# A decoder block in fp32 on one core: V transposed by VectorE instead of TensorE, and a seven-product block multiplication that sums in PSUM

## The chip, the cores and the metric

The kernel runs on one core of one Trainium2 chip. The metric is device time in microseconds for one launch that computes the whole block; lower is better. The core has five engines with instruction queues of their own: TensorE (PE, with its weight loads shown apart as PEld), VectorE (DVE), ScalarE (ACT), GpSimd (POOL) and SyncE (SP), which here does nothing but issue transfers. Each engine works through its own queue in order, and waits on semaphores for the others.

## What is computed

One decoder block on a sequence of 2048 positions with 1024 channels, everything float32. The largest part is one input projection into 9216 columns; its columns are q, k and v of a dilated attention in three groups, several gates, and the input of a linear recurrence (RG-LRU).

```python
proj = x @ w_in[l] + b_in[l]                       # (2048 x 1024) @ (1024 x 9216)
q, k, v, g_attn, u_lru, g_lru, gate_logits = jnp.split(proj, SPLIT_POINTS, axis=-1)
q = rope(...); k = rope(...)
for g, (window, dilation) in enumerate(DILATION_GROUPS):
    o_g, lse_g = dilated_band_attention(q[:, :, g], k[:, :, g], v[:, :, g], window, dilation)
...
y_a = (attn * silu(g_attn)) @ w_attn_proj[l]
h = rg_lru(causal_depthwise_conv(u_lru, ...), ...)
y_b = (h * jax.nn.silu(g_lru)) @ w_lru_proj[l]
merged = gates[:, :, 0] * y_a + gates[:, :, 1] * y_b
x = layer_norm(DEEPNORM_ALPHA * x + merged @ w_out[l] + b_out[l], ...)
```

## The kernel before

The program has three stages, one after the other. Stage A is the input projection, stage B the attention, stage C the three output products and the normalisation. The change lies in stage A.

**Number format.** Every fp32 operand of a product is split into a high and a low part (`h`, `l` for weights, planes 0 and 1 of the activation blocks `XB`), and each block product is three passes, high by high, high by low, low by high.

**Quads and products.** Stage A takes the 72 column tiles of 128 in 36 pairs, and the sequence in two halves of two chunks of 512 positions (`CH`). One pair in one half is a *quad*; there are 72. In a quad a 2x2 block of weights meets a 2x2 block of activations, with seven block products instead of eight (Strassen's scheme in Winograd's form), called M1 to M7 below after the numbers of `UNIT` and `BLK`. Only the first quad of each half multiplies plainly, with eight. A block product is one *tick*: `product(s, j)` issues 12 matmuls of 128x128 by 128x512 into one PSUM bank. `MID`, `EDGE` and `FIRST` give the order of the seven in a quad. All 506 ticks are issued by one loop, and this loop writes the order of all engines by hand: in each tick the product, then the `events` due (loads, splitting of weights three or four ticks ahead in `prep_w`, sums of weights), then delayed pieces (`late`), then steps of the chains, and last `evacuate(s, j)`, which deals with the bank just finished.

**Sums of the products.** The four results of a quad are, up to signs, M1+M2, U2+M5+M3, U2+M7+M5 and U2+M7+M4 with U2 = M1-M6. In the kernel before, each product has a bank to itself (tag `q`, four banks), ACT copies M1 to SBUF as `e`, and DVE makes everything else: `u2 = e - M6`, `u3 = u2 + M7`, then in `result` and `total` the four results (`y`, or `ub` for the recurrence), and once more `u2 = u2 + M5`. The banks of a quad are read by seven DVE instructions.

**Chains.** What happens to a result is a generator that advances by steps, each step once its engine has time left by a planner's account (`Ask`, `spend`, `COST`). `qk_chain` turns q and k; its four small transfers `sw` (line 307) swap partition quarters, and for the third group q is written at line 341 in pieces of 32 numbers, 128 bytes. `v_chain` has to turn V from channels on partitions to positions on partitions. It asks PE for four transposes against an identity matrix (`turn`, line 358) into a PSUM tile `vtp` (tag `t`, two banks); they are issued in the middle of a product, by `pe_later`. Three ticks on, ACT copies the tile to one of two SBUF buffers `vs` (line 366), and a tick later SP stores it with one transfer (line 370) to `v_scr`, in pieces of 128 numbers. There are 48 such chains, four in each of 12 quads. Stage B reads `v_scr` back with positions on partitions.

The eight PSUM banks of stage A are four `q`, two `t` and two `g` (gates of the recurrence).

**End of stage A.** The last quad also issues the first loads of stage B, in the slots that its blocks free: `first` (keys and queries of unit 0, in the slots of M1's and M2's blocks), `second` (unit 1, in those of M6 and M4), `firstv` (V, in that of M7).

Of the kernel before, what the change touches and what calls it, by code (L numbers as in the profile page):

```python
# [8 lines left out]
F32 = mybir.dt.float32  # L9
# [22 lines left out]
def hybrid_block_kernel(ctx: ExitStack, tc: tile.TileContext, a: dict, out: bass.AP):  # L32
# [89 lines left out]
    MID, EDGE, FIRST = (1, 6, 7, 5, 2, 4, 3), (1, 2, 6, 7, 4, 5, 3), (1, 2, 3, 6, 7, 5, 4)  # L122
# [89 lines left out]
    def hi_lo(n, kk, src, eng=dve):  # L212

        t = XB[n][:, kk]
        act.activation(t[:, 0], src, AF.Copy)  # L215
        eng.tensor_tensor(out=t[:, 1], in0=src, in1=flat(t[:, 0]), op=ALU.subtract)
# [131 lines left out]
    vs_free = [sl_p.tile([P, 4, P], F32, name=f"vs{j}") for j in range(2)]  # L348
    tog = {"n": 0}

    def v_chain(vt, sgn, f, c):
        g, hp = divmod(f - FT_V, 4)
        st = {}

        def turn():
            tp = st["tp"] = ps.tile([P, 4, P], F32, tag="t", name=f"vtp{f}_{c}", bufs=2)
            for b in range(4):
                pe.transpose(tp[:, b, :], flat(vt)[:, b * P:(b + 1) * P], ident)  # L358
            give(vt)

        yield Ask(cond=lambda: tog["n"] < 2)
        tog["n"] += 1
        pe_later(2, turn)
        yield Ask(lag=3, cond=lambda: len(vs_free) > 0, ACT=.66)
        vs = vs_free.pop(0)
        act.activation(vs, st["tp"], AF.Copy, scale=sgn)
# [3 lines left out]
        sp.dma_start(dst.rearrange("(b p) f -> p b f", p=P), vs)  # L370
        vs_free.append(vs)
# [26 lines left out]
    def silu_chain(y, sgn, f, c):  # L398
# [3 lines left out]
        act.activation(y, y, AF.Identity, scale=0.25 * sgn, bias=bq[:, f:f + 1])  # L402
# [153 lines left out]
    for h in range(2):  # L556
        for p, (kind, f0, f1) in enumerate(seq):
            plan.append((h, ((f0, kind), (f1, kind)), None if p == 0 else EDGE if p == len(seq) - 1 else FIRST if p == 1 else MID, p, kind))
    NQ = len(plan)
    ticks = [8 if pl[2] is None else 7 for pl in plan]  # L560
    base = [sum(ticks[:s]) for s in range(NQ + 1)]
# [45 lines left out]
    def product(s, j):  # L607
# [8 lines left out]
        bank = Q["b"]  # L616
# [975 lines left out]
```

## Time and profile before

| | us |
|---|---|
| median of 3 runs | 2104.6 (2103.72 to 2107.59) |
| profiled execution, first to last instruction (span) | 2101.9 |
| profiled execution's own time outside the span | not given; the median lies 2.7 above the span |
| first matmul of stage A starts | 5.97 |
| stage A ends on PE (first scores of stage B) | 1443.70 |
| busy in the span: PE, DVE, ACT, POOL | 2086.3, 1662.7, 1116.7, 493.1 |

Of the profile these views are used: the page, with its busy times and the chain that ended last; the waits, which say for each engine whom it waited for and how long in total; groups of instructions by line with busy time and mean duration; the timeline, where each row is a start, a duration, an engine and what it did, equal neighbours merged (x2 is two of them); and one tile's or one line's instructions with the least, median and largest duration. Matmuls are pipelined: the duration of one is longer than the distance to the next, so their cost is read from the distances of starts. Line numbers are those of the kernel before.

### The profile page before, as it was taken

The page shows a single profiled execution, that of the slowest core. Times are in us where ns is not written, and L with a number is a line of the kernel's source. Part 1 is how long each engine was busy: PE and PEld are TensorE (multiplying, and loading weights), DVE is VectorE, ACT ScalarE, POOL GpSimd, SP SyncE. Part 2 cuts the span into 40 slices and gives each one's busy share as a digit, 9 for nine tenths or more (in the row PEclk, how much of TensorE's full clock was granted, in tenths as well). Part 3 has the DMA queues.
Part 4 walks back from the last instruction along what each step waited for, and adds up shares of the span by engine and source line. Part 5 has one row for each costly group of instructions (what it writes and reads, how often), then busy time and mean ns, then how long its engine had stood idle before and what let it go on. Part 6 is the DMA issues. An engine that isn't in the chain of part 4 may idle for free.

```text
span 2101.9 us, 35814 instructions
## 1 busy us (share of the span) xinstructions
PE 2086.3 (99%) x12016; PEld 1726.9 (82%) x12016; DVE 1662.7 (79%) x3179; ACT 1116.7 (53%) x2341; POOL 493.1 (23%) x468
## 2 busy tenths in 40 slices
PE   8999999999999999999999999999999999999998
PEld 7888888888888888888888888888999888888887
DVE  8987888889988867787877888877999645576667
ACT  6455456457457565666666775766999411211100
POOL 1111111110111011231221222222545344431120
PEclk9999999999999999999999999999999999999999
DMA  8987997987997967777779778769996788864432
GB/s 271 276 261 225 274 285 216 282 283 235 278 294 242 332 208 204 231 227 220 225 254 278 254 252 266 252 219 374 355 359 236 228 296 281 298 224 160 154 105 71
DMA packets 327160, 524.69 MB, mean 250 GB/s; under 512 B 105536, under 2 KB 135232, under 8 KB 323136
## 3 DMA queue, kind: packets, MB, share of 16 engines
q1 hardware_dynamic: 307088, 489.54, 70.5%
q0 software_dynamic: 12256, 19.42, 5.5%
q10 hardware_dynamic: 7632, 13.44, 1.7%
q8 instruction: 96, 1.57, 0.3%
q14 instruction: 88, 0.72, 0.1%
HBM read 317.14 MB, written 190.45 MB: 241 GB/s over the span
## 4 chain that ended last, share of the span: by engine, by line
PE 91%; DVE 3%; DMA 3%; ACT 2%; issue 1%; SPq 0%; DVEq 0%; ACTq 0%
PE q L622 66%; PE yb L1340 3%; PE yb L1341 3%; PE z L1451 3%; PE yb L1342 3%; PE z L1450 3%; PE z L1452 3%; ACT p L1023 2%; DVE p L1015 2%; PE ya L1419 1%; PE ya L1418 1%; PE ya L1420 1%; PE g L492 1%; PE vtp L358 1%; DMA B<-k_scr 1%; DMA o_scr<-ot 1%
## 5 line engine op out<-in xcount | busy, mean ns | idle before, releaser
L622 PE MATMUL q<-xT,hS 128*128 128x512 f32 x1680 | 521.0, 391 | 0.0
L622 PE MATMUL q<-xT,l 128*128 128x512 f32 x1120 | 436.0, 389 | 0.0
L622 PE MATMUL q<-xB,hA 128*128 128x512 f32 x1248 | 388.9, 393 | 6.0 <-ACT xB L215 6.0
L622 PEld LDWEIGHTS q<-xT,hS 128*128 128x128 f32 x1680 | 312.9, 188 | 69.0 <-issue 5.5
L622 PE MATMUL q<-xB,l 128*128 128x512 f32 x904 | 352.9, 390 | 0.0
L622 PEld LDWEIGHTS q<-xB,hA 128*128 128x128 f32 x1248 | 233.8, 189 | 57.3 <-ACT xB L215 6.0
L622 PEld LDWEIGHTS q<-xT,l 128*128 128x128 f32 x1120 | 210.2, 188 | 44.1
L622 PEld LDWEIGHTS q<-xB,l 128*128 128x128 f32 x904 | 170.3, 188 | 36.0
L245 POOL DMA_DIRECT2D wS<-in_w_in_dram x70 | 61.9, 950 | 491.5 <-DMA wS<-in_w_in_dram 140.0
L622 PE MATMUL q<-xB,hS 128*128 128x512 f32 x560 | 174.0, 392 | 0.0
L1023 ACT ACTIVATE p<-p,sta 128x256 f32<-128x256 f32 (+1 forms) x384 | 172.7, 469 | 1.2 <-PE pt L1034 0.8
L622 PE MATMUL q<-xT,hA 128*128 128x512 f32 x560 | 173.0, 390 | 0.0
L269 ACT ACTIVATE hA<-wA 128x512 fp32r<-128x512 f32 x218 | 134.9, 623 | 54.4 <-DMA wA<-in_w_in_dram 24.9
L269 ACT ACTIVATE hS<-S 128x512 fp32r<-128x512 f32 x175 | 109.0, 623 | 79.3 <-DVE S L227 49.0
L227 POOL TENSOR_TENSOR S<-S,wA 128x512 f32<-128x512 f32 x35 | 45.5, 1301 | 391.8 <-DVE S L227 208.8
L622 PEld LDWEIGHTS q<-xT,hA 128*128 128x128 f32 x560 | 104.7, 188 | 23.0 <-issue 1.5
L622 PEld LDWEIGHTS q<-xB,hS 128*128 128x128 f32 x560 | 104.0, 188 | 22.4 <-issue 1.5
L1015 DVE CUSTOM_DVE_ANT_0 p<-s,mask 128x256 f32<-128x256 f32 (+1 forms) x384 | 116.4, 360 | 0.2 <-PE s L1008 0.2
L1451 PE MATMUL z<-wo,mh 128*128 128x512 f32 (+1 forms) x264 | 101.0, 383 | 0.0
L1452 PE MATMUL z<-wo,ml 128*128 128x512 f32 (+1 forms) x264 | 101.0, 383 | 0.0
L1450 PE MATMUL z<-wo,mh 128*128 128x512 f32 (+1 forms) x264 | 101.0, 383 | 0.0
L227 DVE TENSOR_TENSOR l<-wA,hA 128x512 fp32r<-128x512 f32 x113 | 79.3, 702 | 26.9 <-ACT hA L269 26.6
(204 smaller groups left out, 4257.0 us busy)
## 6 DMA issues: line engine op xcount, KB each, us to landing
wA<-in_w_in_dram SPq DMA_DIRECT2D x253, 256.0 KB, 4.7
wl_scr<-l SPq DMA_DIRECT2D x105, 512.0 KB, 5.2
l<-wl_scr SPq DMA_DIRECT2D x105, 512.0 KB, 4.6
sw<-y SPq DMA_DIRECT2D x384, 64.0 KB, 3.2
wS<-in_w_in_dram SPq DMA_DIRECT2D x70, 256.0 KB, 4.8
wS<-in_w_in_dram POOLq DMA_DIRECT2D x70, 256.0 KB, 6.3
qh_scr<-hi SPq DMA_DIRECT2D x48, 256.0 KB, 5.5
v_scr<-vs SPq DMA_DIRECT2D x48, 256.0 KB, 4.4
```

What stands on the lines that cost most here:

```text
L227: eng.tensor_tensor(out=out, in0=in0, in1=in1, op=op)
L245: pool.dma_start(t, w_part(s, x), accum_op=ALU.add)
L269: act.activation(h, r, AF.Copy)
L622: pe.matmul(bank, w[:, ks], x[:, kk, xx], start=(first and i == 0), stop=(last and i == 11))
L1015: dve.tensor_tensor_reduce(out=st["p", i, j][:, h, lo:256], in0=st["s", i, j // 2][h][:, j % 2, lo:256], in1=mask[:, lo:256], scale=1.0, s ...
L1023: act.activation(p, p, AF.Exp, scale=-1.0, bias=s[:, h:h + 1], accum_out=s[:, 2 + h:3 + h])
L1340: pe.matmul(yb, WL[f][:, 0, k], xx[:, 0], start=(k == 0), stop=False)
L1341: pe.matmul(yb, WL[f][:, 0, k], xx[:, 1], start=False, stop=False)
L1342: pe.matmul(yb, WL[f][:, 1, k], xx[:, 0], start=False, stop=(k == 7))
L1450: pe.matmul(z, mh[:, k], w[:, 0, hs], start=(k == 0), stop=False)
L1451: pe.matmul(z, mh[:, k], w[:, 1, hs], start=False, stop=False)
L1452: pe.matmul(z, ml[:, k], w[:, 0, hs], start=False, stop=(k == 7))
```

## The change

Three things change.

1. V is turned by VectorE. `v_chain` now transposes the result tile in 32x32 blocks with one DVE instruction into `vs`, without PE, PSUM or ACT. Since each block is turned in its own place, the store puts the blocks in order: four transfers for each V tile, one for each quarter of the partitions, in pieces of 32 numbers. So that no sign has to be applied on the way, the block T2 is negated when it is split, which makes U2 = M1+M6, and signs and biases of other results follow (`silu_chain`, `consts`).
2. Sums of the products are accumulated in PSUM. A quad has four banks, `BANK` A to D: M1, M6 and M5 all accumulate in A, M7 and M4 in C; M2 has B and M3 has D. ACT copies A to SBUF three times, as `e` after M1, `u` after M6 and `v` after M5. DVE makes just the four results. The tag `q` has six banks, `t` none.
3. The order is 1, 2, 6, 7, 3, 5 and then, in the next quad after its first two products, 4. Only the last quad of each half has all seven, as 1, 2, 6, 7, 5, 3, 4. `where` is this list of ticks, still 506. Two results of a quad are made in `between`, in the tick after M5's. Loads at the two halves' border, and the first loads of stage B in the last quad, move with it.

```diff
-    MID, EDGE, FIRST = (1, 6, 7, 5, 2, 4, 3), (1, 2, 6, 7, 4, 5, 3), (1, 2, 3, 6, 7, 5, 4)
+    ORDER, LAST = (1, 2, 6, 7, 3, 5, 4), (1, 2, 6, 7, 5, 3, 4)
+    BANK = {1: "A", 2: "B", 6: "A", 7: "C", 5: "A", 3: "D", 4: "C"}
...
+        if n == "T2":
+            act.activation(t[:, 0], src, AF.Copy, scale=-1.0)
+            dve.scalar_tensor_tensor(out=t[:, 1], in0=src, scalar=-1.0, in1=flat(t[:, 0]), op0=ALU.mult, op1=ALU.subtract)
+            return
...
-        pe_later(2, turn)
-        yield Ask(lag=3, cond=lambda: len(vs_free) > 0, ACT=.66)
+        yield Ask(cond=lambda: len(vs_free) > 0, DVE=.72)
         vs = vs_free.pop(0)
-        act.activation(vs, st["tp"], AF.Copy, scale=sgn)
-        tog["n"] -= 1
+        dve.transpose(vs, flat(vt))
+        give(vt)
         yield Ask()
-        dst = v_scr[g][hp // 2][c * CH:(c + 1) * CH, (hp % 2) * P:(hp % 2) * P + P]
-        sp.dma_start(dst.rearrange("(b p) f -> p b f", p=P), vs)
+        dst = v_scr[g][hp // 2][c * CH:(c + 1) * CH].rearrange("(b i) f -> i b f", i=32)
+        for a in range(4):
+            f0 = (hp % 2) * P + 32 * a
+            sp.dma_start(dst[:, :, f0:f0 + 32], vs[32 * a:32 * a + 32].rearrange("p (b f) -> p b f", f=32))
...
+        js = list(range(8 if pl[3] == 0 else 7 if pl[3] == len(seq) - 1 else 6))
+        own = [(s, j) for j in js]
+        where += own[:2] + ([(s - 1, 6)] if pl[3] > 1 else []) + own[2:]
...
-            n, x, first, last, end = UNIT[order[j]], XB[BLK[order[j]]], True, True, True
+            n, x, last, end = UNIT[order[j]], XB[BLK[order[j]]], True, True
+            first = order[j] in (1, 2, 7, 3)
+        b = s, BANK[order[j]] if order else "P"
         if first:
-            Q["b"] = ps.tile([P, CH], F32, tag="q", name=f"q{j}_{s}", bufs=4)
+            Q[b] = ps.tile([P, CH], F32, tag="q", name=f"q{j}_{s}", bufs=6)
...
+        if pid in (1, 6, 5):
+            n = {1: "e", 6: "u", 5: "v"}[pid]
+            Q[s, n] = take(f"{n}{s}", F32)
+            act.activation(Q[s, n], b, AF.Copy)
...
-        elif pid == 6:
-            Q["u2"] = take(f"u{s}", F32)
-            tt(dve, Q["u2"], Q["e"], b, ALU.subtract)
-        elif pid == 7:
-            Q["u3"] = take(f"v{s}", F32)
-            tt(dve, Q["u3"], Q["u2"], b, ALU.add)
-        elif pid == 5:
-            result(s, 1, c1, b, Q["u3"])
-            tt(dve, Q["u2"], Q["u2"], b, ALU.add)
...
+    def between(s, j):
+        order = plan[s][2]
+        if not order:
+            return
+        b = order.index(5)
+        if j == b:
+            result(s, 1, 2 * plan[s][0] + 1, Q[s, "C"], Q[s, "v"])
+        if j == max(b, order.index(3)):
+            result(s, 0, 2 * plan[s][0] + 1, Q[s, "D"], Q[s, "v"])
+            give(Q.pop((s, "v")))
...
-            for fn in ((), first[:2], first[2:], second[:2], firstv, second[2:], ())[j]:
+        if T >= base[NQ - 1]:
+            for fn in ((), first[:2], first[2:], (), second[:2], firstv, (), second[2:])[T - base[NQ - 1]]:
```

In the three places below the rows are the built program's, in program order; `q5_4` is the bank of the product at place 5 of quad 4, `y25_1` the result of column tile 25 in chunk 1, and the last number of a name is a running one. What a row waits for stands in brackets.

PE, before, in the last product of quad 4 (M3, bank `q6_4`): the four transposes of one V tile stand between its sixth and its seventh matmul.

```order
L622 MATMUL q6_4_1237<-xB22_365,hS4_4_1153 128x512 x2
L622 MATMUL q6_4_1237<-xB22_365,l6_4_1155 128x512
L358 MATMUL vtp25_1_1244<-ident_180,y25_1_1181 128x128 [waits DVE_49,Pool_49]
L358 MATMUL vtp25_1_1244<-ident_180,y25_1_1181 128x128 x3
L622 MATMUL q6_4_1237<-xB22_365,hS4_4_1153 128x512 x2
L622 MATMUL q6_4_1237<-xB22_365,l6_4_1155 128x512
```

PE, after, from the end of M2 of quad 3 to the start of its M6: M4 of quad 2 stands between them.

```order
L623 MATMUL q1_3_878<-xB21_297,l0_3_768 128x512
L623 MATMUL q3_2_775<-xT4_587,hA22_2_732 128x512 [waits DVE_49]
L623 MATMUL q3_2_775<-xT4_587,hA22_2_732 128x512
L623 MATMUL q3_2_775<-xT4_587,l6_2_734 128x512
...
L623 MATMUL q0_3_851<-xT2_429,hS2_3_820 128x512 [waits Activation_49]
L623 MATMUL q0_3_851<-xT2_429,hS2_3_820 128x512
L623 MATMUL q0_3_851<-xT2_429,l2_3_822 128x512
```

No transpose is left on PE. M4 accumulates in bank C (`q3_2`) and waits for DVE's reading of it; M6 accumulates in bank A (`q0_3`) and waits for ACT's copy.

DVE, before, in quad 4: the bank readings that make `v`, a result and `u`.

```order
L227 TENSOR_TENSOR v4_1159<-u4_1138,q2_4_1140 128x512 [waits DVE_49,PE_49]
L227 TENSOR_TENSOR S4_5_1174<-S2_5_1157,wA12_5_1095 128x512 [waits DMAHW2_49,DVE_49]
L227 TENSOR_TENSOR l0_5_1178<-wA11_5_1064,hA11_5_1176 128x512 [waits DMAHW1_49,Activation_49]
L568 SCALAR_TENSOR_TENSOR y25_1_1181<-q3_4_1161,bn_196,v4_1159 128x512 [waits DVE_49,PE_49]
L227 TENSOR_TENSOR u4_1138<-u4_1138,q3_4_1161 128x512
```

DVE, after, for the same quad: two results, and the transposes of the V tiles.

```order
L567 SCALAR_TENSOR_TENSOR y25_1_1249<-q3_4_1161,bn_196,v4_1228 128x512 [waits DVE_49]
L567 SCALAR_TENSOR_TENSOR y24_1_1251<-q4_4_1182,b72_193,v4_1228 128x512 [waits DMAHW5_49]
L232 TENSOR_TENSOR l4_5_1245<-wS1_5_984,hS1_5_1268 128x512 [waits Activation_49]
L359 STREAM_TRANSPOSE vs1_220<-y25_1_1249 128x512 [waits DVE_49]
L359 STREAM_TRANSPOSE vs0_219<-y24_1_1251 128x512 [waits DMAHW3_49,DMAHW2_49,DMAHW4_49,DMAHW1_49,DVE_49]
```

The sums `u` and `v` are gone from DVE, and a transpose waits for the four stores that last read its buffer.

SP, before, the stores of two V tiles with the weights around them.

```order
L234 DMA wA12_6_1287<-in_w_in_dram 128x512 [waits DMAHW7_49,DVE_49]
L282 DMA wl_scr5_122<-l2_5_1228 128x1024 [waits DMAHW0_49,DVE_49]
L370 DMA v_scr00_75<-vs0_219 128x4x128 [waits DMAHW1_49,Activation_49]
L370 DMA v_scr00_75<-vs1_220 128x4x128 [waits DMAHW2_49,Activation_49]
L282 DMA wl_scr5_122<-l4_5_1285 128x1024 [waits DMAHW3_49,DVE_49]
```

SP, after, the store of one V tile there, and what follows it.

```order
L287 DMA wl_scr4_121<-l4_4_1066 128x1024 [waits DMAHW0_49]
L365 DMA v_scr00_75<-vs0_219 32x16x32 [waits DMAHW1_49,DVE_49]
L365 DMA v_scr00_75<-vs0_219 32x16x32 [waits DMAHW2_49]
L365 DMA v_scr00_75<-vs0_219 32x16x32 [waits DMAHW3_49]
L365 DMA v_scr00_75<-vs0_219 32x16x32 [waits DMAHW4_49]
L239 DMA wS1_6_1177<-in_w_in_dram 128x512 [waits DMAHW5_49]
```

Each V tile is four issues on SP, and the next quads' weights stand behind them in the same queue.

More of the change, by code (lines that the diff above doesn't have):

```diff
@@ L621, in product @@
             for w, xx in ((h, 0), (h, 1), (l, 0)):
-                pe.matmul(bank, w[:, ks], x[:, kk, xx], start=(first and i == 0), stop=(last and i == 11))
+                pe.matmul(bank, w[:, ks], x[:, kk, xx], start=(first and i == 0), stop=(last and i == 11),
+                          skip_group_check=not first and order is not None)
                 i += 1
@@ L755, in hybrid_block_kernel @@
     E0 = base[len(seq)] - 7
-    for t, b, c in ((2, "B11", 2), (3, "B21", 2), (6, "B12", 3), (7, "B22", 3)):
+    for t, b, c in ((2, "B11", 2), (3, "B21", 2), (6, "B22", 3), (7, "B12", 3)):
         bring(E0 + t, b, c)
@@ L925, in hybrid_block_kernel @@
     low = NS
-    where = [(s, j) for s in range(NQ) for j in range(ticks[s])]
     for T, (s, j) in enumerate(where):
```

58 lines of the change are left out of this document (20 added, 38 removed).

## The prediction

> **What bounds the kernel now.** I read the page first, then the chain that ended last, then whom PE waited for, then stage A by engine.
>
> ```profile
> span 2101.9 us, 35814 instructions
> PE 2086.3 (99%) x12016; PEld 1726.9 (82%) x12016; DVE 1662.7 (79%) x3179; ACT 1116.7 (53%) x2341; POOL 493.1 (23%) x468
> PEclk9999999999999999999999999999999999999999
> PE 91%; DVE 3%; DMA 3%; ACT 2%; issue 1%; SPq 0%; DVEq 0%; ACTq 0%
> PE q L622 <- ACT xB L215: 6.0, 1, 6.0
> PE s L1008 <- DVE sta L1015: 0.5, 2, 0.3
> 0.00:722.00 722.00, 716.03 (x3206) 586.57 (x3207) 623.42 (x1002) 392.79 (x651) 97.63 (x127) 1.00 0.88 267
> 722.00:1444.00 722.00, 722.00 (x3258) 587.48 (x3256) 561.38 (x787) 459.55 (x745) 164.08 (x137) 1.00 0.77 243
> ```
>
> Four lines are of the page, two are PE's longest waits (total, times, longest), two are the halves of stage A: stretch, length, then busy time of PE, PEld, DVE, ACT, POOL, then granted clock, DMA share and GB/s. PE is busy 99% of the span and makes 91% of the chain; in stage A it waits once, 6.0 us at the very start, and its clock is granted in full. So PE's stream of instructions is the time: what is taken from it is gained, what makes it wait is lost. DVE is next, 86% busy in the first half and 78% in the second.
>
> **Transposes leave PE.** The first of them in the timeline (start, duration), and the group of all:
>
> ```profile
> 104.47 0.39 PE L622 MATMUL q<-xB,l 128*128 128x512 f32 x1
> 105.15 0.39 PE L622 MATMUL q<-xB,l 128*128 128x512 f32 x1
> 105.39 0.60 PE L358 MATMUL vtp<-ident,y 128*128 128x128 f32 x4
> 106.29 0.40 PE L622 MATMUL q<-xB,l 128*128 128x512 f32 x1
> L358 PE MATMUL vtp<-ident,y x192: 270/272/273, 105.4 to 1099.1; 128*128 128x128 f32 x192
> ```
>
> Without transposes two `l` matmuls start 0.68 us apart (104.47 to 105.15), with four of them between 1.14 (105.15 to 106.29): 0.46 us for each V tile, or 48 x 0.46 = 22.1 us. Nothing hides them, as PE never rests. The last row's 272 ns are a duration, and durations overlap: four of them in a row would be 1.09 us, more than twice what the starts show. The Trainium skill (TensorE: Matmul & The Clock Gate, Part 4: PE-mode transpose) gives about 275 ns for such a transpose inside a kernel; the trace agrees with that duration. Taken as the price, it would make the gain 192 x 0.275 = 52.8 us, an estimate from that page.
>
> **The wait that the accumulation adds.** M6 writes where ACT reads `e`, M5 where ACT reads `u`, M4 where DVE reads M7. Before, a bank came round after four products; now PE must not return to it until it is read. In a quad two products lie between each pair, 2 x 2.72 us (a product is four times 0.68), so a reading may be 5.4 us late at no cost. There are exceptions: the first seven-product quad of each half has no M4 to put in, so M6 comes 2.72 us after M1. In the first half this falls into the start:
>
> ```profile
> 33.30 0.62 PE L622 MATMUL q<-xB,hA 128*128 128x512 f32 x2
> 36.02 0.62 PE L622 MATMUL q<-xB,hS 128*128 128x512 f32 x2
> 37.15 0.58 ACT L645 ACTIVATE e<-q 128x512 f32<-128x512 f32 x1
> ```
>
> M1 ends where M2 begins, at 33.30; the third product starts at 36.02, and that is now M6. ACT is behind with four splittings of T1 and copies `e` only from 37.15 to 37.73. PE waits 1.7 us, 1.8 with the signal. The same four splittings stand ahead of the copy in the new order, so I take 1.8; the ends are 0 and 2.7.
>
> In the other quads a wait arises only when ACT is held for over 5.4 us. Who holds it (total, times, longest):
>
> ```profile
> ACT e L645 <- PE q L622: 84.6, 27, 7.2
> ACT hi L335 <- DVE rp L227: 36.3, 14, 8.1
> ACT ubs L600 <- DVE y L568: 27.8, 4, 7.5
> ACT hA L269 <- DMA wA<-in_w_in_dram: 24.9, 14, 5.6
> ACT hA L269 <- DVE l L227: 10.5, 7, 5.9
> ```
>
> The first row says that 27 of the 70 copies had ACT waiting ready; before the other 43 it was busy or held elsewhere. The four others are holds with a longest over 5.4: by 2.7, 2.1, 0.2 and 0.5, together 5.5 us if each meets a copy once. Lower end 0, upper 5.5; I take 2.2, since three of the four are waits for DVE, which gets lighter. The last quad of each half has one product between M5 and M4 for ACT's copy and DVE's reading (0.6 and 0.75 us); I take 0.5 for both, ends 0 and 2 x 2.7.
>
> **DVE and ACT, beside PE.** Groups (busy us, mean ns):
>
> ```profile
> L227 DVE TENSOR_TENSOR u<-e,q 128x512 f32<-128x512 f32 x70 | 47.7, 682 | 27.2 <-PE q L622 27.1
> L227 DVE TENSOR_TENSOR v<-u,q 128x512 f32<-128x512 f32 x70 | 47.7, 681 | 25.1 <-PE q L622 25.0
> L227 DVE TENSOR_TENSOR u<-u,q 128x512 f32<-128x512 f32 x70 | 47.4, 676 | 0.0
> L645 ACT ACTIVATE e<-q 128x512 f32<-128x512 f32 x70 | 41.1, 588 | 93.3 <-PE q L622 84.6 <-POOL sw L227 6.4 <-DMA mg_scr<-y 2.2
> L366 ACT ACTIVATE vs<-vtp 128x512 f32<-128x512 f32 x48 | 27.6, 589 | 30.4 <-DMA v_scr<-vs 14.1 <-PE vtp L358 12.4 <-PE q L622 3.9
> L1075 DVE COPY ot<-o 128x512 f32<-128x512 f32 x4 | 2.7, 687 | 0.0
> L527 DVE TENSOR_TENSOR_SCAN h<-tr,hst,sq 128x512 f32<-128x512 f32 x32 | 41.8, 1305 | 2.0 <-PE q L622 1.9
> ```
>
> DVE loses the three `u`/`v` sums, 142.8 us, and gains 48 transposes that no row prices. Nearest are a copy of the same size, 0.69 us, and the scan, 1.31; I take the copy, 33 us (ends 33 to 63). Net about -110 of 1185 us. ACT gains 140 copies at 0.588 and loses 48 at 0.589: +54 us on 852, 63% of stage A. Neither touches the end while PE leads. Negating T2 costs eight instructions a few hundredths more: nothing.
>
> A transpose waits until its buffer's last store has landed; the transposes have two buffers as before, but the wait now stands on DVE, and behind it stand splittings of weights and bank readings. ACT's old wait for these stores was the 14.1 us above. Stores now land later (below); I take twice that, 28 us, upper end 48 x 4.4 = 211, against 259 + 110 us in which DVE is free. Weights are split three to four ticks, 8 to 11 us, before PE needs them: nothing.
>
> **Stores: one becomes four, in 128-byte pieces.** The same amount in the same pieces is already written for q of the third group, at line 341:
>
> ```profile
> L341 SPq DMA_DIRECT2D ql_scr<-rp x16: 2115/2678/5558, 77.8 to 1294.4; - x16
> DMA to landing us min/median/max: 4.2/5.7/11.1
> L370 SPq DMA_DIRECT2D v_scr<-vs x48: 365/384/1181, 106.6 to 1105.0; - x48
> DMA to landing us min/median/max: 2.3/4.4/7.7
> L307 SPq DMA_DIRECT2D sw<-y x384: 507/588/1542, 61.5 to 1390.1; - x192
> wA<-in_w_in_dram SPq DMA_DIRECT2D x253, 256.0 KB, 4.7
> ```
>
> Line 341 holds SP 2.68 us instead of 0.38 and lands after 5.7 us instead of 4.4. So each V tile takes SP 2.3 us more, 9.2 in a V quad of 19 us. Behind it wait the next weights. But a quad of q and k issues 16 `sw` at 0.588, 9.4 us, and for the third group line 341 besides, and PE waited for none of it; V quads have no `sw` of their own. I take 0 for PE. The Trainium skill (DMA: Bandwidth & Descriptors, Specifications) speaks against the change: under 512 bytes a transfer is read, modified and written. The trace agrees in direction, 2.68 against 0.38 us. If that rule set the time here it would be rival 2.
>
> **Moved loads.** At the end of stage A, unit 1's queries (two issues of SP) now wait for M4, the very last product; before:
>
> ```profile
> 1446.26 0.33 SPq L826 DMA_DIRECT2D A<-ql_scr  x1
> A<-ql_scr SPq DMA_DIRECT2D x12, 1024.0 KB, 10.8
> 1459.90 1.53 PE L1008 MATMUL s<-B,A 64*128 64x128 f32 x23
> ```
>
> The later of the two was issued at 1446.26, after stage A anyway, and landed by 1457.1; unit 1 starts at 1459.90, 2.8 us later. Issued at the stage's end, 1443.7, both land within some 11 us, against 16 us to unit 1's start: 0. At the halves' border block B12 is split one tick later, four ahead of its use: 0.
>
> **Sum.** -22.1 (transposes) + 1.8 (start) + 2.2 (late copies) + 0.5 (last quads) = -17.6 us. Against the span, 2101.9 - 17.6 = 2084.3; the median stands 2.7 above the span, so 2104.6 - 17.6 = 2087.0 us. All lower ends: 2082.5; all upper: 2104.6 - 22.1 + 2.7 + 5.5 + 5.4 = 2096.1.
>
> **Rivals.**
> 1. Bank waits eat the gain. For it: 43 late copies of 70, and M4 needs ACT, then DVE, in turn. Against: 5.4 us of room, and DVE gets lighter. If DVE's backlog in the busier half makes each of its 35 quads wait 0.5 us beyond the start's 1.8: 2104.6 - 22.1 + 1.8 + 17.5 = 2101.8, no change. It decides at 0.5 us a quad.
> 2. Slower: V's stores hold back the weights behind them. A weight issued four ticks (10.9 us) ahead and landing after 4.7 has 6.2 us to spare; if SP's extra 9.2 us of a V quad fall on it in one piece, PE loses 3.0 us in each of 12: 2104.6 - 17.6 + 36 = 2123.0. Break-even is 1.5 us a V quad. For it: ACT already waits for `wA`, 14 times. Against: the quads of q and k above.
> 3. The transposes cost PE their full duration, 1.09 us a tile: 2104.6 - 52.2 + 4.5 = 2056.9. For it: the row's 272 ns. Against: the starts, 0.46 a tile. The Trainium skill's figure, named above (TensorE: Matmul & The Clock Gate, Part 4), is nearly this duration.
> 4. That PE's work isn't taken away is excluded: the new order holds no transpose on PE, and as many products.
>
> **How the numbers follow.** Forecast 0.82, rival 1 0.07, rival 2 0.07, rival 3 0.02, other gains 0.02. The range goes from 2081 (all lower ends, less a little for waits that a lighter DVE ends) to 2099, past all upper ends and into mild forms of rival 1; about 0.8 lies in it. Under 0.2%, 4.2 us, a measurement of this kernel can't be told from no change. Faster 0.86 (forecast, rival 3, other gains), same 0.07 (rival 1), slower 0.07 (rival 2).
>
> **What would show it.** Right: stage A ends on PE 17 to 20 us earlier, at about 1426; the distance of `l` matmuls is 0.68 throughout; PE's waits show 1 to 2 us for ACT's copy near 36 us and a few us elsewhere; DVE falls by about 110 us in stage A, ACT rises by about 54. Wrong: PE waits for ACT's copies or for DVE's result in most quads (rival 1), or for weights in V quads, with SP's line 365 long (rival 2); or a DVE transpose far over 1.3 us, so that DVE becomes the bound.

## The result and the profile after

| | before | after |
|---|---|---|
| median, us | 2104.9 | 2123.9 (2121.86 to 2124.28) |
| ratio | | 1.0087 [1.0075, 1.0099] |
| profiled execution, span, us | 2101.9 | 2122.3 |
| first to last product matmul of stage A, us | 1437.4 | 1448.2 |
| the rest of the span, us | 664.5 | 674.1 |

The change made the kernel 0.9% slower; 2087.0 had been forecast. The third and fourth rows are worked out from the starts of the first and the last matmul of line 623 (622 before). They split the loss in two: 10.8 us in stage A, 9.6 behind it.

Of the page of after: the busy times, the packets, the queue of SP, and the chain that ended last. The fence behind it has the packets and the queue of before.

```profile
span 2122.3 us, 35089 instructions
PE 2077.5 (98%) x11824; PEld 1710.2 (81%) x11824; DVE 1609.3 (76%) x3018; ACT 1159.4 (55%) x2431; POOL 515.1 (24%) x468
DMA packets 403189, 524.65 MB, mean 247 GB/s; under 512 B 206144, under 2 KB 211264, under 8 KB 399168
q1 hardware_dynamic: 383120, 489.55, 72.9%
PE 75%; DVE 7%; ACT 6%; DMA 6%; issue 3%; SPq 2%; POOL 0%; DVEq 0%; ACTq 0%
```

```profile
DMA packets 327160, 524.69 MB, mean 250 GB/s; under 512 B 105536, under 2 KB 135232, under 8 KB 323136
q1 hardware_dynamic: 307088, 489.54, 70.5%
```

PE has 192 instructions less and is busy 8.8 us less, in a span that is 20.4 longer. The bytes are the same, the packets under 512 B have nearly doubled. PE makes 75% of the chain instead of 91%; DVE, ACT, DMA and SP have come onto it. Whom PE waited for (total, times, longest), and the two halves of stage A (PE, PEld, DVE, ACT, POOL busy, clock, DMA share, GB/s):

```profile
PE q L623 <- DVE y L567: 9.5, 6, 2.1
PE s L1007 <- DVE sta L1014: 8.7, 3, 8.3
PE q L623 <- ACT xB L220: 5.6, 1, 5.6
PE q L623 <- DVE y L232: 4.8, 5, 1.1
PE q L623 <- DMA l<-wl_scr: 1.9, 1, 1.9
PE q L623 <- ACT e L648: 1.7, 1, 1.7
0.00:722.00 722.00, 703.02 (x3069) 569.35 (x3070) 570.46 (x908) 404.14 (x681) 99.44 (x127) 1.00 0.90 263
722.00:1444.00 722.00, 714.04 (x3153) 577.33 (x3152) 556.38 (x713) 486.06 (x800) 182.54 (x135) 1.00 0.82 242
```

Before, PE waited once in stage A. Now it waits for DVE's readings of M7's bank (`y`, lines 567 and 232, all ahead of M4; with one reading of `ub` these are 12 waits, 17.6 us by the starts of the matmuls), and at the start of stage B for DVE once more, 8.3 us. DVE became lighter by 53 us in the first half (623.4 to 570.5), but only by 5 in the second (561.4 to 556.4). One of its groups there, before and after (busy, mean ns):

```profile
L227 DVE TENSOR_TENSOR wA<-wA,wA 128x512 f32<-128x512 f32 x35 | 27.9, 796 | 0.0
L232 DVE TENSOR_TENSOR wA<-wA,wA 128x512 f32<-128x512 f32 x35 | 38.4, 1098 | 0.0
```

The same 35 additions take 0.3 us more each; the last section says what ran beside them.

One of the long waits, in the timelines of after (start, duration, in brackets the idle time before and what ended it). SP, DVE, ACT, PE:

```profile
222.09 2.52 SPq L365 DMA_DIRECT2D v_scr<-vs  x4
226.23 4.89 SPq L365 DMA_DIRECT2D v_scr<-vs  x8
231.16 1.07 SPq L239 DMA_DIRECT2D wA<-in_w_in_dram  x1
226.57 0.71 DVE L359 STREAM_TRANSPOSE vs<-y 128x512 f32<-128x512 f32 x1 [5.53 <-DMA v_scr<-vs]
231.84 0.75 DVE L567 SCALAR_TENSOR_TENSOR y<-q,bn,v 128x512 f32<-128x512 f32 x1
224.40 0.60 ACT L648 ACTIVATE v<-q 128x512 f32<-128x512 f32 x1 [4.22 <-PE q L623]
232.64 0.73 PE L623 MATMUL q<-xT,hA 128*128 128x512 f32 x2 [2.15 <-DVE y L567]
```

ACT copied `v` at 224.40, in time. DVE could not read M7's bank then: it stood 5.53 us ahead of a transpose whose buffer was still being stored, and had seven instructions queued ahead of the reading, which came at 231.84. M4 waited for it. Meanwhile SP issued the stores of three V tiles, eight of them in a row; the next weight `wA` left only at 231.16.

The start of stage B in after: the last products on PE, the last result's store by ACT, DVE's probability tile, PE's scores.

```profile
1453.85 0.39 PE L623 MATMUL q<-xT,l 128*128 128x512 f32 x1
1455.76 0.33 ACTq L381 DMA_DIRECT2D mg_scr<-y  x1
1464.49 0.42 DVE L1014 CUSTOM_DVE_ANT_0 p<-s,mask 128x256 f32<-128x256 f32 x1 [8.13 <-DMA mg_scr<-y]
1465.66 1.99 PE L1007 MATMUL s<-B,A 64*128 64x256 f32 x12 [8.27 <-DVE sta L1014]
```

DVE waits 8.13 us to write a probability tile until the last result has left its slot. PE, idle for as long, then works at half clock for a while (0.81 on the mean of 1444 to 1470 us, shown below). The program keeps a list for this, `LATE = [7, 8, 9, 10, 11, 12, 13]`: results of the last quad go to slots that stage B uses late. Before, four results were taken in the last quad; now there are seven, since three of the quad ahead of it come later. When the last two ask, only 9 and 10 are left on the list and both are in use, so the very last result falls into slot 1, where the third probability tile will lie.

### The profile page after: what moved, and what is told of

The parts are those of the page before. It is cut to its first block, busy times and chain, and to the rows that moved or that the text cites. A ratio compares the mean times of both kernels' runs of the same rounds, so it can differ in the third digit from the quotient of the medians.

```text
span 2122.3 us, 35089 instructions
## 1 busy us (share of the span) xinstructions
PE 2077.5 (98%) x11824; PEld 1710.2 (81%) x11824; DVE 1609.3 (76%) x3018; ACT 1159.4 (55%) x2431; POOL 515.1 (24%) x468
## 4 chain that ended last, share of the span: by engine, by line
PE 75%; DVE 7%; ACT 6%; DMA 6%; issue 3%; SPq 2%; POOL 0%; DVEq 0%; ACTq 0%
PE q L623 49%; PE yb L1339 3%; PE z L1451 3%; PE yb L1341 3%; PE yb L1340 3%; PE z L1449 3%; PE z L1450 3%; ACT p L1022 3%; DMA wA<-in_w_in_dram 2%; PE o L1063 1%; PE ya L1419 1%; PE ya L1417 1%; PE ya L1418 1%; PE s L1007 1%; DVE p L1014 1%
## 5 line engine op out<-in xcount | busy, mean ns | idle before, releaser
L623 PE MATMUL q<-xT,hA 128*128 128x512 f32 x560 | 178.2, 400 | 15.7 <-DVE y L567 9.5
L232 POOL TENSOR_TENSOR S<-S,wA 128x512 f32<-128x512 f32 x35 | 58.0, 1656 | 458.4 <-DVE S L232 269.6
L648 ACT ACTIVATE v<-q 128x512 f32<-128x512 f32 x70 | 41.7, 596 | 140.8 <-PE q L623 130.6
L1450 PE MATMUL z<-wo,mh 128*128 128x512 f32 (+1 forms) x264 | 101.0, 383 | 0.0
```

The costliest lines, as they stand in the source:

```text
L232: eng.tensor_tensor(out=out, in0=in0, in1=in1, op=op)
L623: pe.matmul(bank, w[:, ks], x[:, kk, xx], start=(first and i == 0), stop=(last and i == 11), skip_group_check=not first and order is not None)
L1450: pe.matmul(z, mh[:, k], w[:, 1, hs], start=False, stop=False)
```

## The experiments

Eighteen more kernels were run. A is the time from the first to the last product matmul of stage A, R the rest of the span, both from the profiled execution (before 1437.4 and 664.5). One kernel's executions scatter by 2 to 8 us, and A is read from one execution each, so differences of 2 us in A mean little. The kernels with wide pieces put the positions of V in another order, so they move the same bytes but do not compute the attention asked for.

| kernel | V turned by, stores | sums | median us | ratio | A | R |
|---|---|---|---|---|---|---|
| after | DVE, 4 small, SP | new | 2123.9 | 1.0087 [1.0075, 1.0099] | 1448.2 | 674.1 |
| border | same | new | 2114.9 | 1.0045 [1.0030, 1.0060] | 1448.8 | 664.6 |
| vslots | same | new | 2113.0 | 1.0038 [1.0023, 1.0052] | 1450.5 | 664.4 |
| m4_four | same | new, M4 after 4 | 2142.5 | 1.0177 [1.0162, 1.0192] | 1471.6 | 664.2 |
| dve_old_sums | same | old | 2119.4 | 1.0068 [1.0053, 1.0083] | 1453.4 | 664.1 |
| pe_new_sums | PE, 1 wide | new | 2119.0 | 1.0070 [1.0055, 1.0085] | 1450.9 | 664.2 |
| wide | DVE, 1 wide | new | 2107.7 | 1.0016 [1.0007, 1.0026] | 1433.1 | 673.4 |
| quarters | DVE, 4 wide | new | 2113.7 | 1.0042 [1.0027, 1.0057] | 1438.8 | 673.4 |
| act_stores | DVE, 4 small, ACT | new | 2187.6 | 1.0400 [1.0385, 1.0416] | 1513.1 | 672.8 |
| m4_four_b | DVE, 4 small, SP | new, repaired | 2115.5 | 1.0050 [1.0035, 1.0065] | 1450.3 | 664.2 |
| spread | same, in 4 ticks | new | 2119.1 | 1.0070 [1.0055, 1.0085] | 1441.6 | 673.5 |
| mix_a | DVE, 4 small, SP | new, repaired | 2115.9 | 1.0047 [1.0030, 1.0063] | 1450.8 | 664.3 |
| mix_b | same, in 4 ticks | new, repaired | 2103.4 | 0.9993 [0.9984, 1.0003] | 1438.5 | 664.0 |
| wide_old | DVE, 1 wide | old | 2093.3 | 0.9944 [0.9929, 0.9959] | 1428.1 | 664.2 |
| wide_mix | DVE, 1 wide | new, repaired | 2089.4 | 0.9926 [0.9910, 0.9943] | 1423.5 | 664.4 |
| pool_mix | DVE, 4 small, POOL | new, repaired | 2100.8 | 0.9984 [0.9975, 0.9993] | 1436.9 | 664.2 |
| half_mix | DVE, 2 SP and 2 POOL | new, repaired | 2098.6 | 0.9971 [0.9961, 0.9981] | 1432.7 | 664.2 |
| half_two | as half_mix | new | 2108.8 | 1.0021 [1.0012, 1.0031] | 1442.2 | 664.4 |
| half_spread | as half_mix, in 2 ticks | new, repaired | 2097.6 | 0.9966 [0.9954, 0.9979] | 1432.8 | 664.7 |

"Small" is 128-byte pieces, "wide" 512. Three theories were at stake: 1 and later 3, that the room between a product and the reading of its bank is too short in itself; 2, that V's stores make weights, and with them ACT and DVE, late; and the late slot, which is apart from both.

**The late slot: border.**

```
-    LATE = [7, 8, 9, 10, 11, 12, 13]
+    LATE = [7, 8, 9, 10, 11, 12, 13, 14, 15]
```

> Only the list of slots for the last results is longer (slots 14 and 15 added), so that the last result, y71_2, no longer lies where the third probability tile of stage B lies. Theory 1 (late readings and a late slot): the wait of 8.3 us at the start of stage B goes, and the 10 us at half clock behind it with it; 2123.9 - 8.3 - 5 = 2110.6, at least 2115.6 if the clock falls anyway; the stalls in stage A stay. Rival (the transfers of V and of the loads fill the queues, DMA share 1.04 at the border): another load takes the place of the wait and the time stays within 3 us of 2123.9.

R fell by 9.5 us, A stayed. Around the border, after and then border (columns as above):

```profile
1444.00:1470.00 26.00, 17.56 (x133) 14.99 (x132) 10.31 (x38) 11.06 (x33) 7.41 (x8) 0.81 1.04 388
1444.00:1470.00 26.00, 25.13 (x277) 21.25 (x277) 18.69 (x72) 18.67 (x62) 7.44 (x8) 1.00 1.04 384
```

The DMA share is 1.04 in both and no other load took the wait's place. The table repeats it: R is 664.0 to 664.7 in fourteen kernels, and 672.8 to 674.1 in five (after, wide, quarters, act_stores, spread); in these five, and in no other, DVE waits 7.5 to 8.2 us for the last result's store ahead of a probability tile.

**DVE's wait for its own stores: vslots.**

```
-    vs_free = [sl_p.tile([P, CH], F32, name=f"vs{j}") for j in range(2)]
-        yield Ask(cond=lambda: len(vs_free) > 0, DVE=.72)
-        vs = vs_free.pop(0)
+        yield Ask(need=1, DVE=.72)
+        vs = take(f"vs{f}_{c}", F32)
...
-        vs_free.append(vs)
+        give_sent(vs)
```

> The transposed V tile goes to one of the common slots, returned two ticks after its store, instead of one of two buffers of its own (their room makes two more common slots). Theory 1: DVE no longer stands 6 us before a transpose (14.7 us in 6 waits fall under 2), so the waits for M4 at 230 and 395 us and for the weights at 392 us go, 2.3 + 2.3 + 0.8 us, and one window of half clock, 1.7: 2123.9 - 7 = 2117, 2112 to 2120. Rival (V's stores in 128-byte pieces hold back the weights on SP and in the queues): the stores are as they were, and the time stays at 2122 to 2126.

The waits for `v_scr` ahead of transposes are gone (14.7 us before), and A did not fall: 1450.5. The gain in the median is the late slot, which moved by chance. So what stood in the timeline at 226.57 was a link that another replaces: DVE now waits 36.9 us for low parts of weights to be stored, 20.9 in after. The median lies in theory 1's range, but for another reason, and the expectation fell.

**Each part alone: dve_old_sums, pe_new_sums.** The first is the kernel before with the new `v_chain` and the signs that it needs; the second the kernel after with the old `v_chain`, five product banks and one for transposes.

> The kernel before with one part of the change alone: V transposed by DVE, four stores of 128-byte pieces; sums, banks and order of the products as before. (Planner: no DVE time is booked for the transpose, since the slots run out otherwise.) Theory 1: this part does what the prediction said, 22.1 us less PE work and no bank that PE waits for: 2104.6 - 22.1 = 2082.5, up to 2088 if DVE's waits for the stores make some weights late. Rival (stores): waits for weights in the V quads eat it, 2100 or more.

> The other part of the change alone: sums in PSUM, M4 in the next quad, but V transposed on PE with one store as before (five banks for the products, one for the transposes). Theory 2: without V's stores PE waits for banks only at the start (1.8 us), at the ends of the halves and some 1 us at half a dozen M4s, and the late slot at the start of stage B stays with its half clock (about 10 us): 2104.6 + 1.8 + 1.8 + 7 + 10 = 2125, of which stage A 2115. Theory 1 (room for M4 too short): stalls as in the changed kernel plus 22 us of transposes: 2140 or more.

PE's waits in dve_old_sums (first three) and pe_new_sums:

```profile
PE q L612 <- DVE u L227: 8.3, 5, 3.2
PE q L612 <- DMA l<-wl_scr: 8.3, 3, 4.9
PE g L482 <- DVE vl L227: 3.6, 3, 1.5
PE q L633 <- DVE y L232: 4.7, 5, 1.3
PE q L633 <- DVE ub L577: 1.9, 3, 1.0
PE q L633 <- ACT e L658: 1.3, 1, 1.3
```

Either part alone makes stage A longer, by 16.0 and 13.5 us; together it is 10.8, not 29.5. With the old sums DVE has the three sums a quad more to do, and its lateness reaches banks (`u`) and gates (`vl`). Theory 1 missed the first by over 30 us. pe_new_sums met theory 2's figure for stage A (13.5 more against some 11); its small waits are at the M4s (nine, 8.2 us by the starts). Of the late slot, which was expected to stay, R shows nothing. This kernel is not quite the new sums alone, since it has a bank less.

**V's stores: wide, quarters, act_stores.**

```
-        for a in range(4):
-            sp.dma_start(dst[:, :, f0:f0 + 32], vs[32 * a:32 * a + 32].rearrange("p (b f) -> p b f", f=32))
+        sp.dma_start(dst.rearrange("(b p) f -> p b f", p=P), vs.rearrange("p (b f) -> p b f", f=P))   # wide
+        for a in range(4): sp.dma_start(..., vs[32 * a:32 * a + 32].rearrange("p (b f) -> p b f", f=P))  # quarters
+            act.dma_start(dst[:, :, f0:f0 + 32], ...)   # act_stores
```

> The changed kernel with V's four stores per tile replaced by one, in 512-byte pieces as in the kernel before; the positions of V land in another order, so this kernel does not compute attention as asked, but it moves the same bytes. Theory 2, formed after dve_old_sums (V's stores occupy SP and the queues; loads of weights and stores of their low parts issued behind them are late, DVE and ACT stand, and PE with them): most of stage A's stalls between 200 and 440 us and near 1130 go, 14 us with their windows of half clock; the late slot at the start of stage B stays: 2104 to 2111. Theory 1 (PE's room for M4's bank is too short by itself): stalls stay, 2118 to 2125.

> Four stores per V tile as in the changed kernel, each of a quarter of the partitions, but in 512-byte pieces (positions of V in another order, attention not as asked). Tells the number of issues from the size of the pieces. If the pieces are what costs: as with one store, 2104 to 2111. If four issues are what costs: as the changed kernel, 2118 to 2125. An issue of SP should take about 0.3 to 0.4 us here, against 0.51.

> The four stores in 128-byte pieces are issued by ACT instead of SP; the result is the full computation. Theory 2a (SP's time, 2.3 us a V tile, holds the weights back): SP is free, ACT has room, 2105 to 2113. Theory 2b (the pieces fill the DMA engines whoever issues them): weights stay late, 2117 to 2125; and if ACT's own queue then stands, more than 2125.

A falls by 15.1 us with one wide store, by 9.4 with four: with the changed kernel's order the small pieces cost 9.4, the four issues 5.7. PE's waits in wide:

```profile
PE s L1005 <- DVE sta L1012: 8.7, 3, 8.3
PE q L621 <- DVE y L232: 3.6, 4, 1.0
PE q L621 <- DVE y L565: 3.5, 4, 1.2
PE q L621 <- DVE ub L565: 2.7, 2, 1.3
```

The waits of over 2 us in stage A are gone; of some 1 us each ten remain ahead of M4, 11.5 us by the starts of the matmuls: these are theory 1's. In quarters an issue took 0.44 us, a little over what was expected. Issuing from ACT is far worse than either form of theory 2 said, and for the reason named at its end:

```profile
ACT hA L274 <- DMA v_scr<-vs: 67.2, 8, 10.9
```

ACT stands with its queue, and with it the copies that PE now waits for. The run tells nothing on SP.

**Room at the banks: m4_four, m4_four_b, mix_a.**

```
-        where += own[:2] + ([(s - 1, 6)] if pl[3] > 1 else []) + own[2:]
+        where += own[:4] + ([(s - 1, 6)] if pl[3] > 1 else []) + own[4:]     # all three
-    ORDER, LAST = (1, 2, 6, 7, 3, 5, 4), (1, 2, 6, 7, 5, 3, 4)
+    ORDER, LAST = (1, 2, 7, 6, 3, 5, 4), (1, 2, 7, 6, 5, 3, 4)               # m4_four_b, mix_a
+    # mix_a: border's list, and (1, 2, 3, 6, 7, 5, 4) in the first seven-product quad
```

> M4 of a quad is issued after four products of the next quad instead of two; nothing else changes. Theory 1: the room between M5 and M4 grows from 5.4 to 10.9 us, PE's waits for DVE's reading of the bank (9.5 + 4.8 + 1.4 us) fall under 2 us, and the half clock at 255 and 399 us goes (2 x 1.7): 2123.9 - 15 - 3.4 = 2105.5, 2102 to 2109. Rival (stores hold back weights): PE's stalls are taken over by waits for l and hA, the time stays above 2118.

> M4 after four products of the next quad, as in m4_four, and M7 now stands before M6 in a quad (1, 2, 7, 6, 3, 5; last quads 1, 2, 7, 6, 5, 3, 4), so that ACT keeps the time of two products for copying M1 before M6 returns to its bank, which m4_four had cut to one. Theory 3 (a bank that is read through ACT and then DVE needs more than two products of room): the eleven waits at M4 in the changed kernel, 16.9 us with two windows of half clock of 1.7 us each, go; the last result also falls into a slot that no probability tile uses, so the wait of 8 us at the start of stage B goes too: 2123.9 - 20 - 10 = 2094, 2090 to 2104. Theory 2 alone (V's stores delay everything): the waits come back at weights (l, hA), 2110 or more.

> The changed kernel with three repairs: the longer list of late slots (border), M4 after four products with M7 before M6 (m4_four_b), and 1, 2, 3, 6, 7, 5, 4 in the first seven-product quad of each half, so that ACT has the time of two products for its copy of M1. Theory 3: 1.8 us less than m4_four_b, about 2092 (2088 to 2102), and no half clock after 12 us before the end. Theory 2 alone: 2108 or more.

PE's longest waits in m4_four and m4_four_b:

```profile
PE q L623 <- ACT e L648: 28.4, 17, 6.2
PE q L623 <- ACT e L648: 11.4, 8, 3.4
PE q L623 <- DMA l<-wl_scr: 6.0, 4, 3.9
```

m4_four came out 33 us above the top of theory 1's range. The waits for M4 vanish as expected, but a longer one takes their place: M4 had stood between M2 and M6, and without it ACT has one product's time to copy M1. m4_four_b mends this and A is 1450.3, as in after: the waits came back at M6 and at low parts of weights, as theory 2 had it. Theory 3 fell where it was tried, on top of V's stores; mix_a, 2115.9 where 2088 to 2102 was expected, says the same.

**Less of a burst: spread, mix_b.** Four stores in four ticks (`yield Ask()` between them), with vslots; mix_b has mix_a's repairs besides.

> As vslots, and V's four stores of a tile are issued in four different ticks instead of at once, so that no eight of them stand back to back on SP. Theory 2a (the burst of 6 us on SP holds the weights): stage A ends 6 us earlier than in vslots, 1450 instead of 1456 us. Theory 2b (the small pieces fill the queues in any order): stage A ends as in vslots, 1455 to 1457. The last result lies in the slot of the fifth probability tile here, which may cost up to 8 us at the start of stage B.

> mix_a with V's tiles in common slots and the stores of a tile in four ticks (spread). If the burst on SP matters beyond the room at M4, 3 to 6 us less than mix_a, 2086 to 2089; if not, the same as mix_a within 2 us.

A falls by 8.9 us against vslots (1441.6), and by 12.3 in mix_b against mix_a. So the burst on SP counts (theory 2a), by more than either expectation gave it; mix_b's 2103.4 is still far from 2086 to 2089, which took mix_a to be near 2092. With the burst gone the repairs bring 3.1 us of A, and the late slot besides, which came back in spread.

**What is left when the pieces are wide: wide_old, wide_mix.**

> The kernel before with V transposed by DVE, old sums, and one store per V tile in 512-byte pieces (positions of V in another order, attention not as asked); against dve_old_sums only the four small-piece stores are gone. Theory 2 (those stores made the 15 us of dve_old_sums): 2104.2 - 22 + 0 to 6 = 2082 to 2088. Rival (the transposes themselves on a DVE that is 86% busy hold PE up): 2095 or more.

> wide (one store per V tile in 512-byte pieces, attention not as asked) with the three repairs of mix_a. wide has 13.5 us of waits for banks in stage A and the late slot at the start of stage B. Theory 3 (room at M4 and at M1's copy): most of both goes, stage A ends at 1424 to 1428 us instead of 1439, 2084 to 2089, the number first forecast. Rival (a late ACT or DVE meets some bank in any order): only the late slot goes, 2096 to 2100.

wide_mix, at 2089.4, is 2.4 us above the number first forecast and just outside its own range; as its waits show, the sum is not quite the forecast's. Its waits in stage A, without the first, and its halves:

```profile
PE q L621 <- DMA l<-wl_scr: 2.9, 3, 1.4
PE q L621 <- ACT e L646: 1.4, 2, 0.8
PE q L621 <- DVE y L232: 1.0, 1, 1.0
PE q L621 <- ACT u L646: 0.8, 1, 0.8
0.00:722.00 722.00, 714.20 (x3148) 583.41 (x3149) 593.00 (x932) 419.77 (x705) 100.60 (x127) 1.00 0.91 273
722.00:1444.00 722.00, 716.65 (x3328) 581.38 (x3328) 547.46 (x758) 488.87 (x830) 182.28 (x143) 1.00 0.79 245
```

Against wide A falls by 9.6 us: theory 3 holds once the stores are light. wide_old misses its upper bound by 5 us; with the old sums two late weights near 1089 and 1114 us, two windows of half clock and later gates remain. The two also show that the new sums by themselves did not pay: with wide stores A is 1428.1 with the old sums, 1433.1 with the new ones, and 1423.5 only when these have their room. In dve_old_sums the stores cost 25.3 us of A (1453.4 to 1428.1), with the new sums 15.1.

**Other queues: pool_mix, half_mix, half_two, half_spread.** All with vslots and border's list; half_two with the changed kernel's order, the others with mix_a's.

```
-            sp.dma_start(...)
+            (sp if a < 2 else pool).dma_start(...)   # half_mix, half_two; pool_mix: pool alone
+    # half_spread: a = 0 on SP and 2 on POOL, yield Ask(), then 1 and 3
```

> The full computation: the repairs of mix_a, V's tiles in common slots, and V's four stores issued by POOL instead of SP (POOL is busy 23% of the span). Theory 2a (SP's time is what the small stores take from the weights): 2088 to 2096. Theory 2b (the small pieces fill the DMA engines whoever issues them): 2101 to 2106. If POOL, which also waits for weights, issues them late, nothing waits for it but the slots.

> As pool_mix, with two of the four stores on SP and two on POOL, at once. Theory 2a: between mix_b and pool_mix, 2092 to 2100. Theory 2b: 2101 to 2106 as well.

> half_mix with the order of the changed kernel put back: M4 after two products of the next quad, 1, 2, 6, 7, 3, 5, and nothing special in the first quads; the longer list of slots, the common slots for V and the stores on two queues stay. Theory 3 (room at the banks is a cost of its own): its waits return, 6 to 10 us, 2104 to 2109. Theory 2 alone (only the stores count): 2097 to 2100 as half_mix.

> half_mix with the four stores of a V tile in two ticks, one on SP and one on POOL in each. If SP's bursts still hold weights and low parts there, 3 to 5 us less than half_mix, 2093 to 2096, since half_mix has some 7 us of waits at 250, 410 and 420 us beside the V quads; if not, 2097 to 2100.

pool_mix, at 2100.8, lies just under theory 2b's range, and half_mix in theory 2a's; each holds a part. half_mix and half_spread compute the whole block and are 0.3% faster than before, the best of these that do; they cannot be told from each other. half_two met theory 3: against half_mix it is 9.5 us of A, the same price of the room as wide against wide_mix. half_spread came out where its second case said: with two queues the bursts no longer matter. Between mix_a, with the burst on SP, and half_mix lie 18.1 us of A; between half_mix and wide_mix 9.2 remain, which no queue took away. They agree with the 9.4 between after and quarters, so the pieces themselves (theory 2b) cost some 9 us, as far as these runs go; half_mix still has four issues a tile where wide_mix has one, and the two were not taken apart there. PE's waits in half_spread, without the first:

```profile
PE q L625 <- ACT e L650: 5.7, 6, 1.6
PE q L625 <- DMA l<-wl_scr: 4.7, 4, 1.9
PE q L625 <- ACT u L650: 2.1, 2, 1.3
```

## Why the prediction was wrong, point by point

Stage A in four kernels that differ in two things, by A: wide stores and room 1423.5 (wide_mix), wide stores without room 1433.1 (wide), small stores on SP with room 1450.8 (mix_a), both faults 1448.2 (after). So the change without its two faults takes 13.9 us from stage A; the small stores give back 27.3 by themselves, the short room 9.6 by itself, both together 24.7. The 13.9 is not the forecast's 17.6: 21.3 are gained by the transposes (below), and wide_mix still has 7.3 us of waits, by starts, at banks and for low parts of weights, where the forecast had 4.5. Behind stage A come 9.6 for the late slot: -13.9 + 24.7 + 9.6 = +20.4 of span.

- **Transposes leave PE, -22.1: right.** In the middle of products, where the transposes stood, PE lost 49.2 us before and 31.7 after (windows of half clock left out), and in the matmul behind them 7.4 and 3.6: -21.3. Rival 3 is out.
- **The start, +1.8: right.** M6 waited 1.83 us at 36 us, for ACT's `e`.
- **Late copies, +2.2: mis-sized.** 10.6 us in wide, with the stores light, at nine M4s (the tenth is the next item's); beside V's stores the repair of the room gains nothing that can be seen (mix_a against after). The step took for lateness only waits of ACT over 5.4 us. But M4 waits for ACT and then for DVE, and DVE reads the bank after what is queued ahead of it: seven instructions, 5 us, in the timeline above. The step's reason for taking 2.2, "DVE, which gets lighter", held in the first half only (next item but one).
- **Last quads, +0.5: too small.** M5 and M4 of the first half's last quad waited 0.83 and 0.95 us.
- **DVE -110, ACT +54 in stage A: too large.** They changed by -54 (1184.6 to 1130.7, to the end of stage A) and +42 (852.3 to 894.3). DVE lost the three sums as forecast, but some of its other instructions took longer (last section); why ACT gained less stays open.
- **Stores, 0 for PE: the step that failed.** 27.3 us by themselves, 15.1 on top of the short room, 25.3 with the old sums. It set one kind of quad against another, each with 9 us of SP, and from PE's not waiting in the one it took that it would not in the other. But the two do not take turns. V's stores come out when their tiles are ready, many of them behind the end of the V quad, and already before the change they stood among the `sw` of q and k:

```profile
223.76 0.38 SPq L370 DMA_DIRECT2D v_scr<-vs  x1
224.27 3.23 SPq L307 DMA_DIRECT2D sw<-y  x4
```

  So the two add up. In after the quads that start at 224.2 and 389.6 us, in which the long waits at 230.1 and 395.8 lie, hold eight and nine V stores and twelve `sw` each: SP issues for 19.9 of 22.2 us and for 21.9 of 24.1. In the same two quads of wide it is 13.9 of 20.0 and 14.9 of 20.3. The step asked whether weights would be late, and they were seldom what PE waited for (1.9 us in after): late loads and buffers held DVE and ACT, and PE waited for those, as in the timeline at 226.57. That the stores cost this is shown by the runs; that it goes by DVE and ACT is read from such places, as no run separates the ways. The issue of 0.51 us and the transposes were priced about right:

```profile
L365 SPq DMA_DIRECT2D v_scr<-vs x192: 303/511/2406, 99.8 to 1114.1; - x192
L359 DVE STREAM_TRANSPOSE vs<-y 128x512 f32<-128x512 f32 x48 | 33.0, 700 | 14.9 <-DMA v_scr<-vs 14.7
```

  The transposes take 33 us and the waits for their buffers 14.7, against 33 and 28 assumed; wrong was only that nothing stood behind them. The Trainium skill (DMA: Bandwidth & Descriptors, Specifications) says that pieces under 512 bytes are read, modified and written; after against quarters, with the same number of issues and the same bytes, agrees in direction, by 9.4 us. No run shows the reading itself.
- **Moved loads, 0: right for the loads, and the border still cost 9.6 us.** The prediction followed the transfers of the last quad but not the slots of its results.
- **The clock** was no term. Three windows of half clock in stage A cost 1.6 us each (below), and the longer one at the border is part of the 9.6.
- **The rivals.** Rival 2, V's stores, is what came: 36 us priced, 27.3 measured (2.3 a V quad, break-even 1.5), through DVE and ACT more than through weights that PE itself waited for. It had 0.07. Rival 1 came too, 17.5 priced and 9.6 measured, without turning the sign. The near agreement of rival 2's number, 2123.0, with the result is partly chance: the late slot, which no case had, is in the result. Of the signs set for the rivals neither came as written: PE waited at 12 of the 70 M4s, not in most quads, and once for a low part of a weight.

## What to carry to other kernels

Of an engine that works in order, ask what is queued ahead of the reading that another waits for, at the busiest place, not how idle it is on the mean; and where two waits lie on one another, expect the repair of the smaller to show nothing until the larger is gone. Here a transposition that saved PE 21 us and wrote in 128-byte pieces gave back more than that through the queue that also brings the weights; spreading these stores over two queues got 18 us back. When results come out in another order or number, look also at whose place their tiles take next.

## What the runs showed of the hardware

The granted clock fell to half in windows of 3.41 us, or two or three of them in a row, behind PE's waits. In the thirteen traces with more than one such window or run of windows ahead of the kernel's end, all of a trace's windows start on one grid of 3.413 us, to 0.01 us; its phase differs from run to run. Laid on this grid, PE's idle time inside one cell of it decides. In the twenty traces, without the last 15 us of each, every cell at full clock with 1.86 us or more idle was followed by a cell at half clock, and none with 1.83 or less was, but for one: 1.26 us in act_stores at 367.3, where the 64-row gate products run. In a cell already at half clock, less was enough to keep it there, 0.68 us in wide_old at 1115.9; that is how runs of two came about. So in after the wait at 251.6 us, with 2.08 us of idle time in one cell, cost a window, and the one at 230.1, with 2.15 us that the grid cuts into 1.03 and 1.12, did not. In a window matmuls start 0.43 us apart instead of 0.23; eight fit, and it costs 1.6 us. The Trainium skill (TensorE: Matmul & The Clock Gate, Part 1) gives a free-running window of 3413 ns, and the traces agree; its section "Why this matters for your kernels" warns of idle gaps over about 3 us, and here 1.9 us in one window are enough.

In stage A, where POOL also adds and multiplies tiles, some of DVE's instructions on 128x512 take 1.5 to 2.2 us instead of 0.68: 35 before, 81 after, nearly all in the second half. Every one of them overlaps a POOL addition or multiplication by over 0.6 us. In after all 81 have both inputs in SBUF and start later than the POOL instruction; the 37 that start earlier stay short, and so do the 18 that have at most one input in SBUF. What DVE had lost in work in that half it got back in duration: above 0.69 us each, the long ones add up to 37 us before and 87 after. It is not the waits that bring the two engines together more often, since wide_mix, nearly without them, has 71; nor the transposes, since pe_new_sums has 85 and wide_old 35. It came with the new sums and their order: before, 91 instructions with at most one input in SBUF, all of them readings of PSUM banks and 32 of them the sums `u` and `v`, ran beside POOL's and took at most 0.75 us. The Trainium skill (SBUF — State Buffer, "Who interferes with whom") says that a DVE instruction with two inputs in SBUF contends with a GpSimd instruction that reads SBUF, and that the later one is blocked; the overlaps agree. No kernel here tried it by itself. One such pair in after:

```profile
972.83 1.77 DVE L399 SCALAR_TENSOR_TENSOR y<-si,y 128x512 f32<-128x512 f32 x1
972.32 1.73 POOL L232 TENSOR_TENSOR sw<-sw,sin 128x512 f32<-128x512 f32 x1
```
